# Mixers of a two-layer streaming encoder: six PSUM banks in one stock, a new task clock and projection order, and one score group for the later tokens

## The chip, the cores and the metric

The kernel runs on one core of one Trainium2 chip. The metric is the device time of one execution in microseconds (us), lower is better. The engines are TensorE (PE in the profile, with its weight loads as PEld), VectorE (DVE), ScalarE (ACT), GpSimd (POOL) and SyncE (SP), which here only issues DMAs. Each engine has its own list of instructions, in the order of the program, with waits on semaphores for the others.

## The reference, cut to what matters

Two layers, each a feed-forward block, a mixer and a second feed-forward block, for 256 prompt tokens and 32 later tokens (positions 512 to 543, with a cache of 512 keys and values). All matrices are fp32.

```python
x = x + 0.5 * swiglu(rmsnorm(x), ffn1)              # 1024 -> 2816 -> 1024
z = rmsnorm(x) @ w_in                               # 1024 -> 2560: q, k, v (4 heads), u, hc, bg, cg
q, k = rope(q), rope(k)
o = diff_attend(q, k, v)                            # softmax(q1 k1) - lam * softmax(q2 k2), times v
y_attn = rmsnorm(o, subln)                          # prompt: chunk mask; later tokens: 512 cached + 32 new keys
y_pool = pool_mix(u); y_conv = bg * short_conv(cg * hc)
x = x + concat(y_attn, y_pool, y_conv) @ w_out      # 1024 -> 1024
x = x + 0.5 * swiglu(rmsnorm(x), ffn2)
```

New keys, values and the states of pool and convolution are outputs too.

## The kernel before

Tokens lie in the free dimension (288 columns: 256 + 32), features in the 128 partitions. Every large product is made in three fp32r matmuls (`mm3`, lines 244 to 251): high weights by high input (L249), low weights by high input (L250), high weights by low input (L251). One such three is called a **triple** below. A block of 128 output features takes 8 triples where 1024 features go in. A mixer is 20 such blocks of w_in (its **projections**: q, k and v of four heads, two u, two hc, two bg, two cg), 160 triples, and then 64 triples of w_out.

Weights come from HBM in **chunks** of 1 MB, two projections each, three buffers deep. Each must be split into a high part (ACT, `wh`) and a low part (DVE, `wl` = raw - wh). In the mixers the split is made in four pieces of 128x512 for a chunk (pieces 0 to 3, each for four triples), one chunk ahead of its use (`split_task`, `chunk`). ACT and DVE share this work with everything else in the mixer.

That else is written as Python generators, **tasks**, that are started when a projection's accumulator is full (`after`): `rope` (four ACT copies `zw` of 32 partitions, z on DVE, zw times sin on POOL, then q or k on DVE), `val` (value times R, two transposes `tpv`, copy `vtk`), `attn_p` for a head (scores `sc`, maxima `nm` on DVE, four exponentials `e` on ACT, difference on DVE, transposes `tpa`, copy `aT`, product `o`, norm, transposes `tpo`, then mh on ACT and ml on DVE), `attn_s` for the later tokens of all heads (scores `scs`, `es_t`, `tps`, `os`), `pool` (`yp`), `conv` and `gate`. Each `yield wait(...)` is a place where the task may be left. A planner at build time sets the order: `main` emits a triple and moves `clock` on by a fixed cost, `poll` issues every task piece whose `ready_at` lies behind the clock, `Costed` charges each ACT, DVE and POOL instruction to a planned time of its engine. So the order of instructions on all engines is fixed when the kernel is built; on the chip, only semaphores decide. `IN_ORDER` gives the order of the projections (0 to 3 q, 4 to 7 k, 8 to 11 v, 12 and 13 u, 14 and 15 hc, 16 and 17 bg, 18 and 19 cg), and a list in the code the order in which w_out takes its eight inputs.

The kernel uses PSUM as eight banks of 128x512. Before, four rotate for accumulators (`ps_a`), two for tasks (`ps_t`), and `ps_s` holds a pair for scores. The feed-forward blocks use the same pools. In the first mixer, `lambdas` (ACT `lam_e`, DVE `nlam`) is issued when the first two projections are done.

Of the kernel before, what the change touches and what calls it, by code (L numbers as in the profile page):

```python
# [43 lines left out]
IN_ORDER = [0, 4, 1, 5, 8, 9, 2, 6, 10, 11, 3, 7, 14, 15, 12, 18, 13, 19, 16, 17]  # L44
# [20 lines left out]
def tile_step(ctx, tc, xT, head, w_gu, w_dn, w_in, w_out, rest, ck, cvp,  # L65
# [99 lines left out]
    def warm_up(n):  # L165

        warm = ps_a.tile([P, 512], F32, tag="acc", name="warm")
        for _ in range(n):
            PE.matmul(warm[:, 0:P], ones, ones, start=True, stop=True)
# [33 lines left out]
    def stats_a():  # L203

        ps = ps_t.tile([P, 512], F32, tag="tp", name="ps_ss")
# [14 lines left out]
    def stats_b(dg):  # L220
        ps = ps_t.tile([P, 512], F32, tag="tp", name="ps_r")
# [5 lines left out]
    def stats_wide():  # L227

        ps = ps_t.tile([P, 512], F32, tag="tp", name="ps_w")
# [23 lines left out]
    def acc_tile():  # L253
        return ps_a.tile([P, 512], F32, tag="acc", name="acc")
# [158 lines left out]
    def mixer(l, g_next):  # L413
        with tc.tile_pool(name="mp", bufs=1) as mp, tc.tile_pool(name="mt", bufs=2) as mt, \
# [24 lines left out]
            free = {"sc": [0.0], "tp": [0.0, 0.0]}  # L439
# [24 lines left out]

            def ready_at(t):
                _, res, _, dep = t[1]
                at = t[0]
                if dep is not None:
                    at = max(at, done.get(dep, never) + LAG)
                return max(at + MARGIN, min(free[res])) if res else at  # L470

            def issue(t, at):
                _, res, cost, _ = t[1]
                if res:
                    slots = free[res]
                    slots[slots.index(min(slots))] = never
# [4 lines left out]
            def release(res):  # L481
                slots = free[res]
                slots[slots.index(never)] = stage[1] + LAG
# [37 lines left out]
            class Costed:  # L521
# [3 lines left out]
                def __getattr__(self, op):  # L525
                    f = getattr(self.eng, op)

                    def call(out, *a, **kw):
                        n = max(a[0].free_size() if a and hasattr(a[0], "free_size") else 0, out.free_size())
                        if self.name == "act":  # L530
                            src = a[0]
                            c = (0.05 if src.space == PSUM else 0.1) + n / 1200.0 + (0.1 if "accum_out" in kw else 0.0)
                            c += sum(0.05 for x in ("scale", "bias") if hasattr(kw.get(x), "free_size"))
                        elif self.name == "dve":
                            c = 0.07 + n / 960.0
                        elif op == "tensor_tensor":
                            c = 0.3 + 0.165 * n if n < 4 else 0.1 + n * 0.0023
# [8 lines left out]
            def main(*a):  # L546
                mm3(*a)
                clock[0] += 0.369
# [29 lines left out]
            def stats():  # L578
                ps = ps_t.tile([P, 512], F32, tag="tp", name="ps_ss")
# [3 lines left out]
                V.tensor_scalar(a, ps[:, 0:3], 1.0 / D, EPS, ALU.mult, ALU.add)  # L583
                r = tmp.tile([P, 3], F32, tag="rs_r", name="rs_r")
# [6 lines left out]
                ps = ps_t.tile([P, 512], F32, tag="tp", name="ps_r")  # L591
# [5 lines left out]
                S.activation(R[0], ps[:, :T], AF.Copy)  # L597

            def rope(acc, h, isk):
# [6 lines left out]
                V.tensor_tensor(z, acc[:, :T], cosR, ALU.mult)  # L606
                G.tensor_tensor(zw, zw, sinR, ALU.mult)
# [11 lines left out]
            def val(acc, h):  # L619
                v = mt.tile([P, SEQ], F32, tag="vT", name="vT")  # L620
                V.tensor_tensor(v, acc[:, :SEQ], R[0][:, :SEQ], ALU.mult)
                V.tensor_tensor(vcat[:, h, :], acc[:, SEQ:T], R[0][:, SEQ:T], ALU.mult)
                nc.sync.dma_start(vT_o[l, h, :, 0:SEQ], v)
                nc.sync.dma_start(vT_o[l, h, :, SEQ:T], vcat[:, h, :])
                yield wait("tp", 0.45)
                tp = ps_t.tile([P, 512], F32, tag="tp", name="tpv")
# [5 lines left out]
                release("tp")  # L632
                mark(("v", h))

            def val_s():
                yield wait("tp", 0.22)
                tp = ps_t.tile([P, 512], F32, tag="tp", name="tpvs")
# [4 lines left out]
                release("tp")  # L642
                mark("vs")

            def attn_p(h):
# [33 lines left out]
                tp = ps_t.tile([P, 512], F32, tag="tp", name="tpa")  # L679
# [5 lines left out]
                release("tp")  # L685
                yield wait(dep=("v", h))
                yield wait("tp", 0.65)
                o = ps_t.tile([P, 512], F32, tag="tp", name="o")
# [6 lines left out]
            def finish(o, s1, n, dst, key):  # L695
# [16 lines left out]
                release("tp")  # L712
                yield wait("tp", 0.22 * n)
                tp = ps_t.tile([P, 512], F32, tag="tp", name="tpo")
# [10 lines left out]
                release("tp")  # L725
                mark(key)

            def attn_s():
                yield wait(dep=("q", 3))
                yield wait(dep=("k", 3))  # L730
                for c in range(2):
                    yield wait("sc", 1.0)
                    sc = ps_s.tile([P, 2, 512], F32, tag="sc", name="scs")
                    r = slice(64 * c, 64 * c + 64)
                    for b in range(2):
                        for h in range(H):
                            PE.matmul(sc[32 * h:32 * h + 32, b, 0:272], qT[h][r, SEQ:T],  # L737
                                      kts[r, h, b * 272:(b + 1) * 272], start=True, stop=True)
                    yield wait()
                    nm = mt.tile([P, 1], F32, tag="nms", name="nms")  # L740
                    V.tensor_reduce(nm, sc[:, :, 0:272], AX.XY, ALU.max)
                    V.tensor_scalar(nm, nm, -0.125, None, ALU.mult)
                    yield wait()
                    S.activation(es_t[:, c, :].rearrange("p (b k) -> p b k", b=2), sc[:, :, 0:272], AF.Exp,
                                 scale=0.125, bias=nm, accum_out=sms[:, c:c + 1])
                    release("sc")
                yield wait()
                fr = mt.tile([P, 1], F32, tag="frs", name="frs")
# [6 lines left out]
                tp = ps_t.tile([P, 512], F32, tag="tp", name="tps")  # L755
# [3 lines left out]
                tp2 = ps_t.tile([P, 512], F32, tag="tp", name="tps2")  # L759
# [3 lines left out]
                release("tp")  # L763
                release("tp")
                yield wait(dep="vs")
                yield wait("tp", 1.5)
                o = ps_t.tile([P, 512], F32, tag="tp", name="os")
# [8 lines left out]
            def pool(acc, g):  # L776
# [6 lines left out]
                V.tensor_tensor(e[:, 2 * HIST + SEQ:], acc[:, SEQ:T], R[0][:, SEQ:], ALU.mult)  # L783
                nc.sync.dma_start(pool_o[l, g, 0], e[:, SEQ:SEQ + HIST])
# [3 lines left out]
                w = mt.tile([P, L], F32, tag="ws", name="ws")  # L788
                w2 = mt.tile([P, L], F32, tag="ws2", name="ws2")
# [20 lines left out]
                yp = ps_t.tile([P, 512], F32, tag="tp", name="yp")  # L810
# [7 lines left out]
                release("tp")  # L818
                mark(("m", 4 + g))

            def times_R(acc, tag):
                t = mt.tile([P, T], F32, tag=tag, name=tag, bufs=1)
                V.tensor_tensor(t, acc[:, :T], R[0], ALU.mult)
                return t

            def conv(acc, g):
# [11 lines left out]
                y = mt.tile([P, L], F32, tag="ws", name="cy")  # L838
# [21 lines left out]
            def after(mi, acc):  # L860
# [12 lines left out]
                elif mi < 16:  # L873
                    hcR[mi - 14] = times_R(acc, f"hcR{mi - 14}")
# [5 lines left out]
            def residual(m, acc):  # L880
                V.tensor_tensor(xs[m], acc[:, :T], xs[m], ALU.add)
                yield wait()
# [16 lines left out]
            a2 = [acc_tile() for _ in range(2)]  # L899
# [13 lines left out]
            for i in range(2, 20, 2):  # L913
# [5 lines left out]
                for q in range(2):  # L919
                    acc = acc_tile()  # L920
# [3 lines left out]
            order = [4, 5, 0, 1, 2, 3, 6, 7]  # L924
            acc4 = [acc_tile() for _ in range(4)]
# [12 lines left out]
            for m in range(4, KD):  # L938
                if m % 2 == 0:
                    w = chunk()  # L940
                acc = acc_tile()
# [3 lines left out]
            finish_tasks()  # L945

    class Close:
# [11 lines left out]
        def sums_before(self):  # L959

            self.ps = ps_t.tile([P, 512], F32, tag="tp", name="ps_l")
# [8 lines left out]
        def finish_all(self, acc):  # L970
# [7 lines left out]
            half = [[acc_tile(), acc_tile()], [acc_tile(), ps_t.tile([P, 512], F32, tag="tp", name="yt_p")],  # L978
# [152 lines left out]
```

## Time and profile before

| what | before |
|---|---|
| median of 3 runs (lowest to highest) | 1077.22 us (1076.9 to 1078.23) |
| the profiled execution: its own time, its span | 1078.57 us, 1076.8 us |
| PE busy | 1064.5 us, 99% of the span |
| DVE, ACT, POOL busy | 698.5 us (65%), 534.2 us (50%), 32.1 us (3%) |
| granted clock of TensorE, mean | 0.998 of full speed |
| DMA | 180.11 MB, mean 167 GB/s |

The span is what the profile sees from the first to the last instruction. Matmuls overlap in the records (each shows about 0.29 us, one starts every 0.13 us), so a matmul's cost is read from starts, and an idle time that the profile shows for PE is less than what PE lost. The two mixers lie around 222 to 312 us and 752 to 842 us.

### The profile page before, as it was taken

To read this page: it belongs to the slowest core of one execution; us is meant where nothing else is said; L and a number is where in the kernel's file an instruction comes from. 1 tells how busy PE (TensorE), PEld (TensorE's weight loads), DVE (VectorE), ACT (ScalarE), POOL (GpSimd) and SP (SyncE) were. 2 spreads that over 40 slices of the span, in tenths; PEclk is the share of its full clock that TensorE was granted. 3 is DMA by queue.
4 is the path that set the end of the run, shared out by engine and by line. 5 is a ranking of instruction groups with operands and counts; after the bars stand their busy time and mean duration, and the time that the engine had idled before them with its cause. 6 is when DMAs were issued, how large, how long until landed. Compare 5 with 4: busy or idle time off the path is not lost.

```text
span 1076.8 us, 19610 instructions
## 1 busy us (share of the span) xinstructions
PE 1064.5 (99%) x8094; PEld 1053.0 (98%) x8094; DVE 698.5 (65%) x1195; ACT 534.2 (50%) x935; POOL 32.1 (3%) x61
## 2 busy tenths in 40 slices
PE   9999999999999999999999999999999999999997
PEld 8999999999999999999999999999999999999997
DVE  6866665557879666655576666554779786666442
ACT  6544444448665444444444444443785644444442
POOL 0000000011200000000000000000112000000000
PEclk9999999999999999999999999999999999999999
DMA  8664444444445444444445444544444364444421
GB/s 284 217 228 177 157 156 171 176 150 169 130 152 215 177 157 161 176 172 157 157 164 184 162 157 166 180 164 166 170 141 157 122 232 170 179 161 157 167 108 44
DMA packets 33417, 180.11 MB, mean 167 GB/s; under 512 B 7696, under 2 KB 10256, under 8 KB 12848
## 3 DMA queue, kind: packets, MB, share of 16 engines
q1 hardware_dynamic: 33328, 178.86, 47.2%
q8 instruction: 63, 1.03, 0.4%
q14 instruction: 26, 0.21, 0.0%
HBM read 175.24 MB, written 3.61 MB: 166 GB/s over the span
## 4 chain that ended last, share of the span: by engine, by line
PE 93%; ACT 3%; DVE 2%; DMA 1%; issue 1%; SPq 0%; POOL 0%; ACTq 0%; DVEq 0%; POOLq 0%
PE acc L249 29%; PE acc L251 29%; PE acc L250 29%; ACT zw L541 2%; DMA raw<-in_head 1%; ACT e L541 1%; PE sc L251 1%; PE sc L249 1%; PE sc L250 1%; ACT wh L541 0%; PE scs L737 0%; PE sc L651 0%; PE acc L299 0%; DVE wl L541 0%; PE os L772 0%
## 5 line engine op out<-in xcount | busy, mean ns | idle before, releaser
L249 PE MATMUL acc<-xh,wh 128*128 128x288 f32 x1632 | 487.2, 299 | 0.0
L250 PE MATMUL acc<-xh,wl 128*128 128x288 f32 x1632 | 480.8, 295 | 2.0 <-DVE wl L541 1.9
L251 PE MATMUL acc<-xl,wh 128*128 128x288 f32 x1632 | 480.3, 294 | 0.0
L109 DVE TENSOR_TENSOR wl<-raw,wh 128x1024 fp32r<-128x1024 f32 x258 | 315.7, 1224 | 188.4 <-ACT wh L108 188.0
L108 ACT ACTIVATE wh<-raw 128x1024 fp32r<-128x1024 f32 x258 | 273.1, 1060 | 290.1 <-PE acc L251 262.7
L250 PEld LDWEIGHTS acc<-xh,wl 128*128 128x128 f32 x1632 | 307.8, 189 | 3.9 <-DVE wl L541 3.1
L249 PEld LDWEIGHTS acc<-xh,wh 128*128 128x128 f32 x1632 | 306.7, 188 | 2.5 <-issue 1.4
L251 PEld LDWEIGHTS acc<-xl,wh 128*128 128x128 f32 x1632 | 306.8, 188 | 0.0
L249 PE MATMUL acc<-hh,wh 128*128 128x288 f32 x704 | 208.4, 296 | 0.0
L250 PE MATMUL acc<-hh,wl 128*128 128x288 f32 x704 | 207.7, 295 | 0.0
L251 PE MATMUL acc<-hl,wh 128*128 128x288 f32 x704 | 207.0, 294 | 0.0
L251 PEld LDWEIGHTS acc<-hl,wh 128*128 128x128 f32 x704 | 132.6, 188 | 0.0
L250 PEld LDWEIGHTS acc<-hh,wl 128*128 128x128 f32 x704 | 132.2, 188 | 0.0
L249 PEld LDWEIGHTS acc<-hh,wh 128*128 128x128 f32 x704 | 131.9, 187 | 0.0
L355 ACT ACTIVATE hh<-t 128x288 fp32r<-128x288 f32 x88 | 39.0, 444 | 108.0 <-DVE t L354 108.0
L541 DVE TENSOR_TENSOR wl<-raw,wh 128x512 fp32r<-128x512 f32 x112 | 76.6, 700 | 5.7 <-ACT wh L541 5.6
L541 ACT ACTIVATE wh<-raw 128x512 fp32r<-128x512 f32 x112 | 65.6, 627 | 6.5 <-PE acc L251 4.1
L356 DVE TENSOR_TENSOR hl<-t,hh 128x288 fp32r<-128x288 f32 x88 | 40.2, 458 | 39.7 <-ACT hh L355 39.4
L349 DVE TENSOR_TENSOR t<-acc,R 128x288 f32<-128x288 f32 x82 | 37.5, 457 | 31.6 <-PE acc L251 31.3
L352 ACT ACTIVATE t<-t 128x288 f32<-128x288 f32 x88 | 37.8, 429 | 6.8 <-DVE t L349 6.1
L354 DVE TENSOR_TENSOR t<-t,t 128x288 f32<-128x288 f32 x88 | 39.6, 451 | 0.1
L249 PE MATMUL acc<-mh,wh 128*128 128x288 f32 x128 | 37.9, 296 | 0.0
(215 smaller groups left out, 784.8 us busy)
## 6 DMA issues: line engine op xcount, KB each, us to landing
raw<-in_w_gu SPq DMA_DIRECT2D x85, 1024.0 KB, 4.8
raw<-in_w_dn SPq DMA_DIRECT2D x44, 1024.0 KB, 4.8
raw<-in_w_in SPq DMA_DIRECT2D x20, 1024.0 KB, 4.9
raw<-in_w_out SPq DMA_DIRECT2D x8, 1024.0 KB, 5.0
raw<-in_head SPq DMA_DIRECT2D x6, 528.0 KB, 6.8
kts<-in_ck SPq DMA_DIRECT2D x2, 1024.0 KB, 5.4
cvt<-in_cv SPq DMA_DIRECT2D x2, 1024.0 KB, 7.2
xall<-in_xT SPq DMA_DIRECT2D x1, 1152.0 KB, 9.9
```

Of the source, the lines that this page charges most:

```text
L108: S.activation(wh, src, AF.Copy)
L109: V.tensor_tensor(wl, src, wh.bitcast(F32), ALU.subtract)
L249: PE.matmul(acc, wh[:, b, :], mh, start=first, stop=False)
L250: PE.matmul(acc, wl[:, b, :], mh, start=False, stop=False)
L251: PE.matmul(acc, wh[:, b, :], ml, start=False, stop=last)
L349: V.tensor_tensor(t1, ag[:, :T], R, ALU.mult)
L352: S.activation(t1, t1, AF.Silu)
L354: V.tensor_tensor(h, t1, t2, ALU.mult)
L355: S.activation(hh[j], h, AF.Copy)
L356: V.tensor_tensor(hl[j], h, hh[j].bitcast(F32), ALU.subtract)
L541: return f(out, *a, **kw)
```

## The change

All of it is in the mixers and their planner.

- Six banks (`ps_b`, tags b0 to b5) form one stock. Accumulators, statistics and tasks take the bank that was free earliest (`take`, `taken`) and give it back by name (`release`), accumulators too, in the middle of a task. A task piece may only be planned while a second bank is free (`spare`). Outside the mixers the six are split four and two as before (`turn_of`, `next_bank`).
- The planner's costs are new: 0.4 instead of 0.369 for a triple, and other costs for ACT, DVE and POOL.
- `IN_ORDER` spreads the ropes: k0, v0, q0, hc0, u0, q1, k1, v1, q2, q3, k2, v2, cg0, k3, v3, bg0, u1, hc1, cg1, bg1. w_out takes its inputs as 4, 5, 6, 7, 2, 3, 0, 1.
- `attn_s` makes the scores of both halves of the heads (c = 0, 1) in one group: all 512 cached keys into the score pair, the 32 new keys into two banks of the stock (`scn`), copied by ACT to `sn`. Before, it was two groups, one for each half, each of 2 x 272 keys.
- Some SBUF buffers: one `ws`, `ws2`; `cy` with a buffer for each group.

```diff
-IN_ORDER = [0, 4, 1, 5, 8, 9, 2, 6, 10, 11, 3, 7, 14, 15, 12, 18, 13, 19, 16, 17]
+IN_ORDER = [4, 8, 0, 14, 12, 1, 5, 9, 2, 3, 6, 10, 18, 7, 11, 16, 13, 15, 19, 17]
+OUT_ORDER = [4, 5, 6, 7, 2, 3, 0, 1]
...
-    ps_a = ctx.enter_context(tc.tile_pool(name="ps_a", bufs=4, space=PSUM))
+    ps_b = ctx.enter_context(tc.tile_pool(name="ps_b", bufs=1, space=PSUM))
     ps_s = ctx.enter_context(tc.tile_pool(name="ps_s", bufs=1, space=PSUM))
-    ps_t = ctx.enter_context(tc.tile_pool(name="ps_t", bufs=2, space=PSUM))
...
+            def opening(res):
+
+                return sorted(free[res])[spare[0] if res == "tp" else 0]
...
-                return max(at + MARGIN, min(free[res])) if res else at
+                return max(at + MARGIN, opening(res)) if res else at
...
+            def taken(name):
+                b = bank(got[0], name)
+                held[id(b)] = (got[0], b)
+                return b
+
+            def take(name):
+
+                while min(free["tp"]) >= never:
+                    at, n = min((ready_at(t), n) for n, t in enumerate(tasks))
+                    assert at < never
+                    issue(tasks[n], at)
+                clock[0] = max(clock[0], min(free["tp"]))
+                got[0] = free["tp"].index(min(free["tp"]))
+                free["tp"][got[0]] = never
+                return taken(name)
...
-                            c = (0.05 if src.space == PSUM else 0.1) + n / 1200.0 + (0.1 if "accum_out" in kw else 0.0)
-                            c += sum(0.05 for x in ("scale", "bias") if hasattr(kw.get(x), "free_size"))
+                            c = 0.17 + n / 1200.0 + (0.1 if "accum_out" in kw else 0.0)
...
-                            c = 0.07 + n / 960.0
+                            c = max(0.18, 0.07 + n / 960.0)
...
-                clock[0] += 0.369
+                clock[0] += 0.4
...
+                yield wait("sc")
+                yield wait("tp")
+                tn = [taken("scn")]
+                yield wait("tp", 1.3)
+                tn.append(taken("scn"))
+                sc = ps_s.tile([P, 2, 512], F32, tag="sc", name="scs")
+                for dst, k0, n in ((tn, PAST, DEC), ([sc[:, 0, :], sc[:, 1, :]], 0, PAST)):
+                    for h in range(H):
+                        for c in range(2):
+                            r = slice(64 * c, 64 * c + 64)
+                            PE.matmul(dst[c][32 * h:32 * h + 32, 0:n], qT[h][r, SEQ:T], kts[r, h, k0:k0 + n],
+                                      start=True, stop=True)
+                yield wait()
+                sn = mt.tile([P, 2, DEC], F32, tag="sn", name="sn", bufs=1)
                 for c in range(2):
...
+                    S.activation(sn[:, c, :], tn[c][:, 0:DEC], AF.Copy)
+                    release(tn[c])
+                nm = mt.tile([P, 4], F32, tag="nms", name="nms")
+                V.tensor_reduce(nm[:, 0:2], sc, AX.X, ALU.max)
...
-            acc4 = [acc_tile() for _ in range(4)]
+            order = OUT_ORDER
+            acc4 = [take("acc") for _ in range(4)]
+            spare[0] = 0
```

Three places show how the order of instructions moves; both mixers are alike but for `lam_e`.

**Place 1, ACT at the start of the first mixer**, from the copy of the statistics (R) on. `zw x4` is one rope's share, a `wh` of 128x512 one piece of the next chunks' weights. Before:

```order
L541 ACTIVATE R<-ps_r 128x288
L541 ACTIVATE zw<-acc 32x288 x8
L273 ACTIVATE lam_e<-lam_s 128x4
L541 ACTIVATE wh<-raw 128x512
L541 ACTIVATE zw<-acc 32x288 x4
L541 ACTIVATE wh<-raw 128x512
L541 ACTIVATE zw<-acc 32x288 x4
L541 ACTIVATE wh<-raw 128x512 x3
```

Now, in the same stretch of ACT:

```order
L577 ACTIVATE R<-ps_r 128x288
L577 ACTIVATE zw<-acc 32x288 x4
L284 ACTIVATE lam_e<-lam_s 128x4
L577 ACTIVATE wh<-raw 128x512
L577 ACTIVATE zw<-acc 32x288 x4
L577 ACTIVATE vtk<-tpv 128x2x128
L577 ACTIVATE wh<-raw 128x512 x5
```

Four ropes stood ahead of the fifth piece of weights; now two do, and `lam_e` comes after one rope.

**Place 2, PE at the scores of the later tokens** (the numbers behind q are buffers of the four heads). Before, each mixer has two such groups, one for each half c:

```order
L737 MATMUL scs<-kts,q_2501 32x272
L737 MATMUL scs<-kts,q_2502 32x272
L737 MATMUL scs<-kts,q_2503 32x272
L737 MATMUL scs<-kts,q_2504 32x272
L737 MATMUL scs<-kts,q_2501 32x272
L737 MATMUL scs<-kts,q_2502 32x272
L737 MATMUL scs<-kts,q_2503 32x272
L737 MATMUL scs<-kts,q_2504 32x272
```

Now each mixer has one (x2: the two halves of a head, from partitions 0 to 63 and 64 to 127):

```order
L781 MATMUL scn<-kts,q_2498 32x32 x2
L781 MATMUL scn<-kts,q_2499 32x32 x2
L781 MATMUL scn<-kts,q_2500 32x32 x2
L781 MATMUL scn<-kts,q_2501 32x32 x2
L781 MATMUL scs<-kts,q_2498 32x512 x2
L781 MATMUL scs<-kts,q_2499 32x512 x2
L781 MATMUL scs<-kts,q_2500 32x512 x2
L781 MATMUL scs<-kts,q_2501 32x512 x2
```

The same columns of keys, in matmuls of 512 and 32 columns instead of 272, and the halves now alternate.

**Place 3, ACT after the scores of head 1**, now: the last exponentials of head 1, the rope of q2, piece 1 of chunk 5 (counted from 0; it holds the weights of k2 and v2), the rope of q3, then pieces 2 and 3 of chunk 5 and piece 0 of chunk 6:

```order
L577 ACTIVATE e,sm<-sc,nm 128x128
L577 ACTIVATE e,sm<-sc,nm 128x256
L577 ACTIVATE zw<-acc 32x288 x4
L577 ACTIVATE wh<-raw 128x512
L577 ACTIVATE zw<-acc 32x288 x4
L577 ACTIVATE wh<-raw 128x512 x3
```

Two ropes now stand close together here, each ahead of a piece of weights; before, q2 and q3 were four projections apart.


## Rows read from the trace of the kernel before

**Rows 1.** Page, busy time: us, share of the span, instructions of each engine.

```profile
PE 1064.5 (99%) x8094; PEld 1053.0 (98%) x8094; DVE 698.5 (65%) x1195; ACT 534.2 (50%) x935; POOL 32.1 (3%) x61
```

**Rows 2.** Windows: busy us (instructions) of a feed-forward stretch and a mixer.

```profile
222.00:312.00 90.00, 87.84 (x703) 82.94 (x702) 67.12 (x173) 59.61 (x165) 15.15 (x26) 1.00 0.47 161
312.00:752.00 440.00, 440.00 (x3323) 439.78 (x3323) 280.71 (x415) 201.20 (x285) 0.00 (x0) 1.00 0.47 167
```

**Rows 3.** Timeline of PE, mixer 1: start, us, instruction [idle <-releaser].

```profile
232.34 0.29 PE L251 MATMUL acc<-xl,wh 128*128 128x288 f32 x1
...
234.04 0.40 PE L250 MATMUL acc<-xh,wl 128*128 128x288 f32 x1 [1.07 <-DVE wl L541]
234.28 0.30 PE L251 MATMUL acc<-xl,wh 128*128 128x288 f32 x1
...
238.24 0.29 PE L249 MATMUL acc<-xh,wh 128*128 128x288 f32 x1
...
238.87 0.29 PE L251 MATMUL acc<-xl,wh 128*128 128x288 f32 x1
...
241.79 0.29 PE L249 MATMUL acc<-xh,wh 128*128 128x288 f32 x1
...
242.21 0.29 PE L251 MATMUL acc<-xl,wh 128*128 128x288 f32 x1
243.18 0.71 PE L651 MATMUL sc<-k,q 64*128 64x256 f32 x4 [0.68 <-ACT e L541]
...
255.06 0.29 PE L249 MATMUL acc<-xh,wh 128*128 128x288 f32 x1
...
255.92 0.30 PE L251 MATMUL acc<-xl,wh 128*128 128x288 f32 x1
```

**Rows 4.** Timeline of PE, mixer 2, first lost stretch.

```profile
766.34 0.29 PE L249 MATMUL acc<-xh,wh 128*128 128x288 f32 x1
...
767.02 0.30 PE L251 MATMUL acc<-xl,wh 128*128 128x288 f32 x1
```

**Rows 5.** Waits of PE in 752 to 842 us: us in total, times, longest.

```profile
PE sc L651 <- ACT e L541: 0.7, 1, 0.7
PE acc L250 <- DVE wl L541: 0.5, 2, 0.3
```

**Rows 6.** Timeline of ACT, start of mixer 1.

```profile
227.62 3.32 ACT L541 ACTIVATE zw<-acc 32x288 f32<-32x288 f32 x8
```

**Rows 7.** Timeline of DVE, the same stretch.

```profile
231.20 0.64 DVE L274 TENSOR_TENSOR nlam<-lam_e 128x2 f32<-128x2 f32 x1 [3.44 <-ACT lam_e L273]
...
233.31 0.68 DVE L541 TENSOR_TENSOR wl<-raw,wh 128x512 fp32r<-128x512 f32 x1
```

**Rows 8.** Timeline of PE, a score group of later tokens and their product os.

```profile
277.97 0.29 PE L251 MATMUL acc<-xl,wh 128*128 128x288 f32 x1
278.19 1.12 PE L737 MATMUL scs<-kts,q 64*32 64x272 f32 x16
279.25 0.41 PE L249 MATMUL acc<-xh,wh 128*128 128x288 f32 x1
279.49 0.29 PE L250 MATMUL acc<-xh,wl 128*128 128x288 f32 x1
...
294.85 1.08 PE L772 MATMUL os<-cvt,aTs 128*32 128x128 f32 x32
295.86 0.42 PE L772 MATMUL os<-vsm,aTs 32*32 32x128 f32 x8
```

**Rows 9.** Timeline of DVE, maxima of a prompt head.

```profile
239.63 0.42 DVE L541 MEMSET sc<- 64x128 f32 x2
...
241.14 0.17 DVE L541 TENSOR_SCALAR nm<-nm 128x4 f32<-128x4 f32 x1
```

**Rows 10.** Timeline of ACT, exponentials of that head and four pieces of weights.

```profile
241.41 0.37 ACT L541 ACTIVATE e<-sc,nm 128x128 f32<-128x128 f32 x1 [2.63 <-DVE nm L541]
...
243.01 2.19 ACT L541 ACTIVATE wh<-raw 128x512 fp32r<-128x512 f32 x4
```

More of the change, by code (lines that the diff above doesn't have):

```diff
@@ L74, in tile_step, with bank, next_bank @@
     tmp = ctx.enter_context(tc.tile_pool(name="tmp", bufs=2))
[L75 removed]
+    ps_b = ctx.enter_context(tc.tile_pool(name="ps_b", bufs=1, space=PSUM))
     ps_s = ctx.enter_context(tc.tile_pool(name="ps_s", bufs=1, space=PSUM))
[L77 removed]
+    turn_of = {"acc": [0, 1, 2, 3], "tp": [4, 5]}
+    def bank(i, name):
+        return ps_b.tile([P, 512], F32, tag=f"b{i}", name=name)
+    def next_bank(kind, name):
+        ids = turn_of[kind]
+        ids.append(ids.pop(0))
+        return bank(ids[-1], name)
     chunks = []
@@ L438, in mixer @@
             clock = [0.0]
-            free = {"sc": [0.0], "tp": [0.0, 0.0]}
+            free = {"sc": [0.0], "tp": [0.0] * 6}
+            held = {}
+            got = [0]
+            spare = [1]
             never = 1e9
@@ L479, in issue, with release @@
                 advance(t, at)
-            def release(res):
-                slots = free[res]
-                slots[slots.index(never)] = stage[1] + LAG
+            def taken(name):
[11 more added lines that the diff above has]
+                return taken(name)
+            def release(b):
+                if b == "sc":
+                    free["sc"][0] = stage[1] + LAG
+                else:
+                    free["tp"][held.pop(id(b))[0]] = stage[1] + LAG
             def mark(key):
@@ L578, in stats @@
             def stats():
-                ps = ps_t.tile([P, 512], F32, tag="tp", name="ps_ss")
+                ps = take("ps_ss")
                 for b, (t0, _, _) in enumerate(TB):
@@ L590, in stats @@
                 yield wait()
-                ps = ps_t.tile([P, 512], F32, tag="tp", name="ps_r")
+                ps = take("ps_r")
                 PE.matmul(ps[:, :T], ones, dg, start=True, stop=True)
@@ L730, in attn_s @@
                 yield wait(dep=("k", 3))
-                for c in range(2):
[L732 to L746, printed above, removed]
@@ new lines, in attn_s @@
+                V.tensor_scalar(nm[:, 0:2], nm[:, 0:2], -0.125, None, ALU.mult)
+                yield wait()
+                for c in range(2):
+                    S.activation(es_t[:, c, 0:PAST], sc[:, c, :], AF.Exp, scale=0.125, bias=nm[:, c:c + 1],
+                                 accum_out=sms[:, c:c + 1])
+                release("sc")
+                for c in range(2):
+                    S.activation(es_t[:, c, PAST:], sn[:, c, :], AF.Exp, scale=0.125, bias=nm[:, c:c + 1],
+                                 accum_out=sms[:, 2 + c:3 + c])
@@ L748, in attn_s @@
+                yield wait()
+                V.tensor_tensor(sms[:, 0:2], sms[:, 0:2], sms[:, 2:4], ALU.add)
                 fr = mt.tile([P, 1], F32, tag="frs", name="frs")
@@ L754, in attn_s @@
                 yield wait("tp", 0.87)
-                tp = ps_t.tile([P, 512], F32, tag="tp", name="tps")
+                tp = taken("tps")
                 for b in range(4):
@@ L898, in mixer @@
             w = chunk()
-            a2 = [acc_tile() for _ in range(2)]
+            a2 = [take("acc") for _ in range(2)]
             for q in range(2):
@@ L919, in mixer @@
                 for q in range(2):
-                    acc = acc_tile()
+                    acc = take("acc")
                     for k in range(KD):
@@ L940, in mixer @@
                     w = chunk()
-                acc = acc_tile()
+                acc = take("acc")
                 for k in range(KD):
@@ L945, in mixer @@
             finish_tasks()
+            ids = sorted(range(6), key=lambda i: free["tp"][i])
+            turn_of["acc"], turn_of["tp"] = ids[:4], ids[4:]
     class Close:
```

70 lines of the change are left out of this document (40 added, 30 removed).

## The prediction

> **What bounds the kernel now.** I read the page first: PE is busy for 99% of the span, DVE for 65%, ACT for 50% [rows 1]. Then a table of windows: in a long stretch outside the mixers PE has no idle time at all and starts a matmul every 440.00 / 3323 = 0.132 us (a triple every 0.397 us); in a mixer's 90 us ACT has work for 60 and DVE for 67 [rows 2]. So ACT and DVE have time enough over a mixer as a whole; only their order can make PE wait. The change leaves the triples as they are, so it can win only what PE loses inside the mixers: waits, and the price of task pieces.
>
> What PE waits for is in its timeline. As matmuls overlap in the records, the view of waits shows too little; I take the time from the start ahead of a wait to the start after it, less 0.132 for each step between. Mixer 1 [rows 3]: 232.34 to 234.28 is 1.94 for three steps, 1.54 lost, on low weights from DVE; 238.24 to 238.87, 0.37 lost; 241.79 to 242.21, 0.16; 242.21 to 243.18, 0.97, where the step into a score group without a wait takes 0.22 (277.97 to 278.19, [rows 8]), so 0.75 lost, on the exponentials of head 0, which still hold the score pair; 255.06 to 255.92, 0.60. Sum 3.42. Mixer 2: the first place loses 0.68 - 0.26 = 0.42 [rows 4], and the view of waits has the same 0.7 for the score pair and two short waits for weights [rows 5]; I take the other three places as in mixer 1 (0.16, 0.75, 0.60), sum 1.93. Together **5.35 us**.
>
> Why they arise: at the start ACT copies eight `zw` for two ropes, 3.32 us [rows 6]. In mixer 1 `lam_e` stands behind them, and DVE, in its order, stands at `nlam` for 3.44 us before it may make the low weights that PE needs, from 233.31 on [rows 7]. All five losses fall in the stretch with ropes 0, 4, 1, 5, 2, 6 close together.
>
> **The change part by part.**
>
> *New order of projections, and the planner's costs.* 0.4 for a triple is nearer to the 0.397 of [rows 2] than 0.369 was; with the old one the planner believed that PE comes sooner than it does. I followed the new order by hand with the durations of the rows: a rope's four `zw` 3.32 / 2 = 1.66 [rows 6], a piece of high weights 2.19 / 4 = 0.55, exponentials 243.01 - 241.41 = 1.60 [rows 10], maxima from 239.63 to 241.31, 1.68 [rows 9], low weights 0.68 [rows 7].
>
> Place 1, start of mixer 1: ACT begins the first rope at 227.62 as before, ends it at 229.28, `lam_e` at about 229.5. DVE took 2.11 from `nlam` to the low weights with three rope steps between [rows 7]; now one is there, so they start at the latest at 229.5 + 2.11 = 231.6 and end at 232.3. PE came to these weights at about 232.5 [rows 3], and now has one pair of transposes more ahead of them. The 1.54 (and the 0.42 of mixer 2) is gone, by a margin of 0.2 with this late bound. The third and fourth rope now come at the sixth and seventh projection instead of the third and fourth, so the 0.37, 0.16 and 0.75 lose their cause too: the score group of head 1 now comes 31 triples after that of head 0 instead of 14, and its pair has long been given back.
>
> Place 3 is the tight one. From the start of head 1's scores to the first use of piece 2 of chunk 5, PE has 19 triples, 7.54, and task pieces: scores 1.0, four pairs and threes of transposes 0.8 (an estimate from the column price below), 9.3 in all, and the low weights are wanted one step later, 9.5. The other chain: scores 0.8, maxima 1.68, exponentials 1.60, rope q2 1.66, piece 1 0.55, rope q3 1.66, piece 2 0.55, low weights 0.68, sum 9.2, and some six hand-offs of 0.05 to 0.1 between engines (241.31 to 241.41, [rows 9, 10]), 9.5 to 9.8. So PE waits between nothing and 0.5; I take **0.25 lost in each mixer**, a new wait. In the other chunks I find each piece ready 0.5 us or more before its first triple. Where a DVE instruction now stands waiting for a projection (values, bg), low weights are queued behind it, but for a later chunk. Taken together the new order gives back 5.35 - 0.5 = **4.85 us**; from below, with 1 us of new waits in each mixer, 3.35; from above 5.35.
>
> *Scores of later tokens.* A group cost 277.97 to 279.49, 1.52 less two steps, 1.26 us; a mixer has two, 2.51. For the price of columns: four heads run side by side, a matmul takes two records, so a group is four rounds of 272 columns in 279.25 - 278.19 = 1.06, and os eight rounds of 128 in 1.01 [rows 8]; the line through both is 0.78 ns for a column plus 0.21. The new group has two rounds of 512 if all eight (head, half) run side by side, 1024 columns, 1.01 like os. The new keys add between 0.05 (64 columns) and 0.42 (the short group of os); I take 0.15. With the steps in and out as before (0.09 and 0.11) the group costs 1.36: a saving of 1.16 in a mixer, **2.3 us** in both. If the two halves don't run side by side, four rounds of 512, 1.8, leave 2.2 for the group and a saving of only 0.3. No row shows eight at once; os shows four column places, the prompt scores two row places (four records of 256 columns in 0.71 us, where 4 x 256 x 0.78 ns one after another are 0.80 and the length of the last, [rows 3]), so I take eight. The Trainium skill (TensorE: Matmul & The Clock Gate, the part on packing small matmuls) says that row and column places compose, with a measured gain of 10.6 for sixteen; by it the sum is the same 1.16, and no run here shows it yet.
>
> *Evacuation.* Two copies `sn`, two more exponentials and three more small DVE steps come behind the new group, and both halves' exponentials in one. Between the group and `tps` PE has 15 triples, 6.0 us, and two task pieces; the chain (maxima of 1024 columns, two exponentials of 512 and two of 32, difference) is an estimate of 5 us from the rows of a prompt head (1.68 and 1.60 for 768). It costs nothing while that cover of about 1 us or more holds; without it `tps`, and all main triples behind it on PE, wait.
>
> *The stock of banks.* It adds waits of PE for a bank. A bank is held for 3.2 us by a projection's triples (8 x 0.397), 1.66 by the rope's copies and somewhat more by z, and a projection starts every 3.2 us, so some two of six are in use, plus short tasks. I count nothing, up to 0.5 in a mixer. The new DMA order is harmless as far as I see: loads still wait for a buffer to be split, as before.
>
> **Sum.** 4.85 + 2.3 = 7.15. The profiled execution would go from 1078.57 to 1071.4; it lies 1.35 above the median of the runs, so the median goes from 1077.22 to about **1070.0**.
>
> **The rivals.**
> 1. *The halves of the scores don't run side by side* (speaks for it: the program alternates them, which no row shows; against: place by place they do). 4.85 + 0.6 = 5.45: 1071.8.
> 2. *Waits come back elsewhere.* The work of ACT and DVE is the same, and a hand count of some two hundred instructions can miss a place where a piece of weights stands behind a task. The Trainium skill (TensorEngine Tiling (Array Packing), PSUM bottleneck) warns that a faster TensorE leaves the evacuation of PSUM as the limit; here that is the chain behind the merged scores, and by that rule the saving of the scores would be lost at `tps`. The mechanism: if that chain takes 2 us longer than estimated, PE waits 1 us or more in each mixer, and with as much again for weights 3 us are given back: 1073.
> 3. *Nothing is won*: the planner's order matters less than the total, and 5 us of waits move to other places: within 0.2%, 1075 to 1079. Against: the losses have named causes that the new order removes.
> 4. *Slower: PE waits for banks.* Projections and tasks now take from one stock; where the bank is given back by a DVE or ACT step that stands behind low weights, a projection begins late. It needs 7.15 + 2.2 = 9.35 us, 0.23 for each of 40 projections, before the kernel is slower by 0.2%; at one piece of low weights (0.68) for every second one, 13.6, the time is 1083.7. Against: two or three of six banks in use.
>
> **How the numbers follow.** The forecast has 0.70 (its own range 1068.9 to 1071.3), rival 1 0.08, rival 2 0.13, rival 3 0.06, rival 4 0.03. A change under 0.2% (2.2 us) can't be told from none here, the three runs alone spread over 1.3 us. Faster is the first three, 0.91; same 0.06; slower 0.03. Range: from no new wait and scores at the lower bound (5.35 + 2.5, 1069.4, and 0.6 for what I can't see) to rival 2: 1068.8 to 1073.4.
>
> **What would show it right or wrong.** In the new profile PE should wait for low weights and for exponentials for under 0.5 us in each mixer, the largest of it at piece 2 of chunk 5; one score group of later tokens in a mixer, some 1.2 to 1.4 us from the step before it to the step after; the pace outside the mixers the same 0.132. It is wrong if PE waits at `tps`, at a projection's first matmul (a bank), or if the scores take four rounds.

## The result and the profile after

| | median of the runs | ratio to before, 95% interval | mixer 1 | mixer 2 |
|---|---|---|---|---|
| before | 1077.0 us (1076.9 to 1078.23) | | 109.45 us | 107.97 us |
| after | 1071.79 us (1071.22 to 1072.34) | 0.9949 (0.9935 to 0.9964) | 105.89 us | 105.88 us |

The change saves 5.2 us in the medians. A mixer is measured from the first start of `ps_ss` in it to that of `ps_w` in the feed-forward block behind it; these lengths repeat to about 0.1 us from one profile to the next, so I use them below more than the medians. Measured so, the mixers of before reach to 332 and 860 us, further than the 312 and 842 named above, as the output projection belongs to them. Both mixers together got shorter by 5.65 us.

The page and the windows answer to [rows 1, 2]. First the page of after, then the windows of its two mixers with the stretch between them, then the same two windows of before (length, then busy us and instructions of PE, PEld, DVE, ACT, POOL, granted clock, DMA share, GB/s).

```profile
PE 1061.1 (99%) x8094; PEld 1052.1 (98%) x8094; DVE 696.7 (65%) x1197; ACT 537.0 (50%) x947; POOL 37.3 (3%) x61
```

```profile
220.88:326.77 105.89, 105.45 (x849) 101.76 (x848) 83.62 (x209) 76.72 (x202) 17.73 (x26) 1.00 0.49 159
326.77:746.97 420.20, 420.20 (x3174) 419.99 (x3173) 263.08 (x381) 185.42 (x255) 0.00 (x0) 1.00 0.49 169
746.97:852.86 105.89, 105.63 (x850) 101.69 (x849) 83.50 (x206) 76.62 (x201) 17.74 (x26) 1.00 0.50 160
```

```profile
222.60:332.04 109.44, 107.28 (x849) 102.38 (x848) 84.25 (x208) 75.72 (x196) 15.15 (x26) 1.00 0.44 149
752.25:860.21 107.96, 106.79 (x849) 102.25 (x848) 83.72 (x205) 75.65 (x195) 15.16 (x26) 1.00 0.46 152
```

ACT and DVE have as much to do as before. In both mixers together PE's idle time fell from 3.33 to 0.70 us and its busy time by 2.99. The pace between the mixers is 420.20 / 3174 = 0.132 us, as before.

The two profiled executions differ by more, 1078.57 to 1071.22. Of that, 1.7 us lie ahead of mixer 1, in code that did not change. About 1.0 of it is a wait of PE early in the first feed-forward block, which the profile of before has and that of after has not; the other 0.7 lies ahead of that wait. That wait does not come from the change: the instructions of experiments 4 and 11 are the same, and the profile of 4 has the wait where that of 11 has not. PE's timeline of before:

```profile
30.55 0.75 PE L222 MATMUL ps_r<-rs_d,ones 128*128 128x288 f32 x2 [0.72 <-DVE rs_d L217]
```

All places of [rows 3, 4] have lost their waits. What PE waits for now is nearly all low weights. The view of waits, PE's weight loads, 222 to 330 us, has one row of `acc` behind `wl` (total us, times, longest):

```profile
PEld acc L261 <- DVE wl L577: 0.7, 1, 0.7
```

It is the place the prediction called Place 3: piece 2 of chunk 5, behind head 1's exponentials and the ropes of q2 and q3. PE's timeline there:

```profile
257.61 0.32 PE L260 MATMUL acc<-xh,wh 128*128 128x288 f32 x1
258.36 0.40 PE L261 MATMUL acc<-xh,wl 128*128 128x288 f32 x1 [0.44 <-DVE wl L577]
258.60 0.30 PE L262 MATMUL acc<-xl,wh 128*128 128x288 f32 x1
```

By the prediction's own rule, 0.99 for two steps, 0.73 lost. Counted likewise, with the ends of the matmuls, mixer 1 loses 0.71 here, 0.14 at piece 2 of chunk 7 and 0.06 twice (once of them for `ml`), 0.97 in all; mixer 2 loses 0.39 and 0.41 at pieces 1 and 2 of chunk 5, 0.13 and 0.05, 0.98. No projection waits for a bank, and nothing waits at `tps`.

The one score group of later tokens, which answers to [rows 8], in PE's timeline:

```profile
283.85 0.30 PE L262 MATMUL acc<-xl,wh 128*128 128x288 f32 x1
284.07 0.27 PE L781 MATMUL scn<-kts,q 64*32 64x32 f32 x13
284.16 0.59 PE L781 MATMUL scs<-kts,q 64*32 64x512 f32 x1
...
284.18 1.05 PE L781 MATMUL scs<-kts,q 64*32 64x512 f32 x13
285.16 0.49 PE L730 MATMUL o<-vtk,aT 128*128 128x128 f32 x2
```

From the step before it to the step after it 1.31 us. The 16 records of 512 columns come in two rounds of eight, which start 0.43 us apart (one record takes 0.59, the row of 13 merged ones 1.05): all eight pairs of head and half run side by side.

### The profile page after: what moved, and what is told of

Read it like the earlier page. It is cut to its first block, busy times and chain, and to the rows that moved or that the text cites. A ratio compares the mean times of both kernels' runs of the same rounds, so it can differ in the third digit from the quotient of the medians.

```text
span 1069.4 us, 19633 instructions
## 1 busy us (share of the span) xinstructions
PE 1061.1 (99%) x8094; PEld 1052.1 (98%) x8094; DVE 696.7 (65%) x1197; ACT 537.0 (50%) x947; POOL 37.3 (3%) x61
## 4 chain that ended last, share of the span: by engine, by line
PE 97%; ACT 1%; DMA 1%; DVE 0%; issue 0%; SPq 0%; ACTq 0%
PE acc L260 30%; PE acc L261 30%; PE acc L262 30%; PE acc L310 1%; PE sc L262 1%; PE sc L260 1%; PE sc L261 1%; ACT zw L577 1%; DMA raw<-in_head 1%; PE sc L691 0%; PE sc L310 0%; ACT e L577 0%; PE os L827 0%; PE o L730 0%; ACT wh L577 0%; PE tpv L668 0%
```

## The experiments

"Mixers" are the two lengths defined above; the ratio is to before, with its 95% interval. Where a diff says `-`, that is the changed kernel, unless said otherwise. In experiments 3, 5, 7, 8 and 11 the output projection also asks for the later tokens' product already ahead of inputs 2 and 3, which read it too, and not only ahead of 0 and 1. With the old prices and clock this changes nothing: the kernels of experiments 4 (without it) and 11 (with it) issue the same instructions in the same order.

**1. The old score groups.** In `attn_s`, shortened:

```diff
-                for dst, k0, n in ((tn, PAST, DEC), ([sc[:, 0, :], sc[:, 1, :]], 0, PAST)):
...
+                for c in range(2):
+                    yield wait("sc", 1.0)
...
+                                PE.matmul(sc[32 * h:32 * h + 32, b, 0:272], qT[h][r, SEQ:T],
```

> The changed kernel with the old two score groups of later tokens (each of four rounds of 272 columns, with its own step in and out) in place of the merged one; all else as after the change. The prediction's theory, corrected by the trace of after (the one group costs 1.31 us, and one of 1.26 is saved, less 0.05 for more columns): each mixer gets longer by 1.2 us, the kernel by 2.4, 1074.2. Rival 1 (the two halves don't run side by side, so that merging saves only 0.3 in each mixer): 1072.4. Rival 2 (the chain behind the merged scores costs as much as the merging saves): no change, 1071.8.

1073.6 us, 0.9969 (0.9958 to 0.998); mixers 107.05 and 107.09, longer by 1.16 and 1.21. PE's timeline has the two groups again:

```profile
280.51 1.12 PE L777 MATMUL scs<-kts,q 64*32 64x272 f32 x16
286.56 1.12 PE L777 MATMUL scs<-kts,q 64*32 64x272 f32 x16
```

The 1.16 of the prediction stands; both rivals of this term fall.

**2. Only the new order, on the kernel before.**

```diff
-IN_ORDER = [0, 4, 1, 5, 8, 9, 2, 6, 10, 11, 3, 7, 14, 15, 12, 18, 13, 19, 16, 17]
+IN_ORDER = [4, 8, 0, 14, 12, 1, 5, 9, 2, 3, 6, 10, 18, 7, 11, 16, 13, 15, 19, 17]
+OUT_ORDER = [4, 5, 6, 7, 2, 3, 0, 1]
```

> The kernel before with nothing but the new order of input and output projections; its prices, its clock, its banks and its two score groups are the old ones. The prediction put the whole 4.85 us of waits on order and prices together. If the order does it alone, the mixers get shorter by 2.5 and 1.0 us (3.42 and 1.93 lost before, less about 0.95 of new waits in each), 1073.5. If it needs the true prices too, half or less of that: 1075 to 1077. If it needs the common stock (two banks for tasks are too few in this order), mixers are as long as before or longer.

1072.94 us, 0.9962 (0.9948 to 0.9977); mixers 106.81 and 106.82, together 3.79 shorter than before. With the old prices PE does not wait for low weights at all. What it loses instead is 0.5 at the first score group of later tokens, for exponentials that still hold the pair, and some 0.1 at each of two groups of transposes. PE's timeline:

```profile
279.54 1.12 PE L738 MATMUL scs<-kts,q 64*32 64x272 f32 x16 [0.45 <-ACT e L542]
```

So the order gives 3.79 by itself, on the kernel before, and the merging 2.37 (1.16 + 1.21), on the kernel after. Prices, clock, stock and buffers, the step from here to experiment 1, cost 0.51 (213.63 to 214.14). The sum is 5.65. These shares hold for this order of steps: taken away last, in experiment 4, the new prices and clock cost more.

**3. The banks apart.** Four banks for accumulators in turn, two for tasks:

```diff
-            free = {"sc": [0.0], "tp": [0.0] * 6}
+            free = {"sc": [0.0], "tp": [0.0, 0.0]}
...
-                b = bank(got[0], name)
+                b = bank(4 + got[0], name)
```

> The changed kernel with the banks apart as before: four for accumulators, taken in turn and not planned for, two for tasks; order, prices and scores as after the change. The prediction counted the stock at nothing: within 0.3 us of the changed kernel. If tasks need more than two banks in the new order (the merged scores hold two by themselves), the attention's transposes and products come later, PE waits for the last of them ahead of the output projections, and each mixer gets longer by 0.5 to 2 us, 1073 to 1076.

1088.67 us, 1.0113 (1.0098 to 1.0128); mixers 115.56 and 115.57: 9.7 longer each, worse than either theory. The merged scores take two banks at once, and with only two for all tasks they start at 292.79 instead of 284.07. The output projection then finds its operands late: PE waits 2.30 us for `ml` from DVE, and 11 us later 1.7 us for `on` from ACT, the later tokens' product. PE's timeline, and the granted clock (the number ahead of the DMA share) in two windows behind it:

```profile
292.79 0.27 PE L775 MATMUL scn<-kts,q 64*32 64x32 f32 x13
...
298.67 0.40 PE L262 MATMUL acc<-ml,wh 128*128 128x288 f32 x1 [2.30 <-DVE ml L571]
...
299.70 0.40 PE L260 MATMUL acc<-mh,wh 128*128 128x288 f32 x1
299.90 0.44 PE L261 MATMUL acc<-mh,wl 128*128 128x288 f32 x1
300.14 0.44 PE L262 MATMUL acc<-ml,wh 128*128 128x288 f32 x1
```

```profile
299.70:302.60 2.90, 2.90 (x16) 2.88 (x14) 2.43 (x5) 0.08 (x1) 0.00 (x0) 0.51 0.47 195
310.60:316.50 5.90, 5.84 (x23) 5.67 (x24) 0.68 (x2) 0.01 (x1) 0.00 (x0) 0.50 0.51 178
```

A second loss comes with each of these two waits: in the stretch behind it the granted clock is 0.51 and 0.50, which is 1.2 instead of 2.4 GHz, and a step takes 0.24 us instead of 0.13. Whether the stock is needed without the merged scores was not tried; experiment 2, with the old banks and the old score groups, has no such waits.

**4. The old prices and the old clock.**

```diff
-                            c = 0.17 + n / 1200.0 + (0.1 if "accum_out" in kw else 0.0)
+                            c = (0.05 if src.space == PSUM else 0.1) + n / 1200.0 + (0.1 if "accum_out" in kw else 0.0)
+                            c += sum(0.05 for x in ("scale", "bias") if hasattr(kw.get(x), "free_size"))
...
-                            c = max(0.18, 0.07 + n / 960.0)
+                            c = 0.07 + n / 960.0
...
-                            c = 0.75 + 0.165 * n if n < 4 else 0.15 + n * 0.0026
+                            c = 0.3 + 0.165 * n if n < 4 else 0.1 + n * 0.0023
...
-                clock[0] += 0.4
+                clock[0] += 0.369
```

> The changed kernel with the planner's old prices and its old clock of 0.369 us for a triple; order of projections, stock of banks and scores as after the change. If the order of projections alone gave the waits back, PE's waits stay as they are, 1.0 us in each mixer, and the time is within 0.5 us of the changed kernel's. If the true prices are what keeps the pieces of weights ahead of PE, old waits return: between 1 and 2.5 us in each mixer, 1074 to 1077.

1070.04 us, 0.9935 (0.992 to 0.995); mixers 104.56 and 104.54. No theory had a gain: the waits for weights are gone. At Place 3 ACT now makes a piece of weights ahead of the first rope. ACT's timeline of this kernel:

```profile
252.66 0.21 ACT L578 ACTIVATION_READ_ACCUMULATOR e<-sc,nm 128x1 f32 x1
252.75 0.64 ACT L578 ACTIVATE wh<-raw 128x512 fp32r<-128x512 f32 x1
253.41 1.64 ACT L578 ACTIVATE zw<-acc 32x288 f32<-32x288 f32 x4
255.08 0.63 ACT L578 ACTIVATE wh<-raw 128x512 fp32r<-128x512 f32 x1
255.74 1.64 ACT L578 ACTIVATE zw<-acc 32x288 f32<-32x288 f32 x4
```

And that of after:

```profile
252.60 0.21 ACT L577 ACTIVATION_READ_ACCUMULATOR e<-sc,nm 128x1 f32 x1
252.84 1.65 ACT L577 ACTIVATE zw<-acc 32x288 f32<-32x288 f32 x4
254.51 0.63 ACT L577 ACTIVATE wh<-raw 128x512 fp32r<-128x512 f32 x1
255.17 1.64 ACT L577 ACTIVATE zw<-acc 32x288 f32<-32x288 f32 x4
256.84 1.67 ACT L577 ACTIVATE wh<-raw 128x512 fp32r<-128x512 f32 x3
```

**5. The old clock alone.**

```diff
-                clock[0] += 0.4
+                clock[0] += 0.369
```

> The changed kernel with only the planner's clock put back (0.369 us for a triple instead of 0.4; prices, order, stock and scores as after the change; the later tokens' product is asked for one chunk earlier in the output projections, which only matters if it is late). With both old numbers (prices and clock) the time was 1070.04 and the mixers 104.55 us instead of 105.9. If the old clock is what keeps the pieces of weights ahead of the rope copies: mixers of 104.6, 1070.0. If it is the prices: mixers of 105.9 or longer, 1071.8 or more.

1134.86 us, 1.0538 (1.0522 to 1.0553); mixers 139.08 and 135.54. With the new, higher prices and the slow clock pieces of weights come late all through the mixer, and tasks behind them. PE's weight loads in mixer 1, in the view of waits:

```profile
PEld acc L261 <- DVE wl L577: 10.2, 9, 2.1
PEld o L730 <- DVE ml L577: 4.5, 1, 4.5
```

The waits are not all of the loss. In four stretches of mixer 1, 27 us together, the granted clock is 0.50 as well. The longest of them, in the view of windows:

```profile
311.00:324.60 13.60, 7.65 (x51) 5.07 (x52) 8.36 (x20) 7.46 (x24) 0.69 (x1) 0.50 0.45 154
```

**6. The old prices alone** (experiment 4 without its last edit, the clock).

> The changed kernel with only the old prices put back (clock 0.4 as after the change; order, stock and scores too). If the new prices are what puts a piece of weights behind two ropes: mixers of 104.6, 1070.0. If the clock is: mixers of 105.9, 1071.8. If either of them suffices, both of these runs are at 1070.0; if the place of each piece hangs on small differences of times in the planner, the mixers lie between 104.5 and 107 with no order in it.

1077.11 us, 1.0001 (0.9992 to 1.0011); mixers 108.26 and 108.20. Here no weights are late, but PE comes to tasks before they are ready. PE's waits in mixer 1:

```profile
PE tpa L722 <- DVE e L578: 0.9, 2, 0.6
PE tps L813 <- DVE es_t L578: 0.8, 1, 0.8
PE yp L868 <- DVE pd L578: 0.7, 1, 0.7
```

Neither old number gives what both give: with the one pieces of weights come too late, with the other tasks too early. What counts is prices against clock.

**7. A clock of 0.43, with the new prices.**

```diff
-                clock[0] += 0.4
+                clock[0] += 0.43
```

> The changed kernel with the planner's clock at 0.43 us for a triple, further from the 0.397 that a triple takes than 0.4 is; its prices are the new ones. If what counts is prices against clock (new prices with 0.369 were far too late, old prices with 0.4 too early, both old or both new about right), a clock that is faster by 7% brings every piece forward: behind head 1's exponentials a piece of weights now stands before the rope, the waits for weights go, and the mixers take 104.5 to 105.3 us, 1069 to 1070.6. If it brings too much forward, PE waits for tasks as with the old prices and 0.4: mixers of 107 to 108, 1074 to 1077. If a clock that is true to the chip is best, it is slower than 0.4 in any case.

1069.31 us, 0.9932 (0.9918 to 0.9946); mixers 104.91 twice, without a wait for weights. The clock is further from the true 0.397, and the mixers are 0.98 shorter than after the change: that a clock true to the chip is best falls.

**8. Weights booked 0.6 us earlier**, the rest as after:

```diff
-                        yield wait()
+                        yield (-0.6, None, 0.0, None)
                         S.activation(wh[:, sl, :], src, AF.Copy)
```

> The changed kernel with every piece of high weights booked 0.6 us earlier in the planner; its prices, its clock of 0.4, order, stock and scores are those after the change. Behind head 1's exponentials ACT now makes one piece of weights, then a rope, one piece, and a rope, in place of a rope, one piece, a rope, one piece. If the wait of after is only that piece's place behind the rope (1.66 us), it goes, and the mixers take 104.5 to 104.9 us: 1069.7 to 1070.5. If pieces that come earlier put a task late in their place (scores, transposes or the output projection), the mixers stay at 105.9 or get longer: 1071.8 or more.

1069.56 us, 0.9937 (0.992 to 0.9954); mixers 105.20 and 105.21. The waits for weights are gone, so the piece's place behind the rope was their cause. Some of it is given back, about 0.45 in each mixer, at the output projection, where `mh` and `ml` now come later.

**9. Without GpSimd's product in the ropes.**

```diff
-                G.tensor_tensor(zw, zw, sinR, ALU.mult)
+                charge("pool", 0.15 + T * 0.0026)
```

> The changed kernel without GpSimd's product of zw and sinR in the ropes (part of the computation is left out; the planner still charges it, so the order of everything else is the same). In the trace of after a subtraction for low weights takes 0.68 us, but 0.74 to 0.81, and once 1.14, where it starts while this product runs. If the subtraction waits there until the product has ended, all of them take 0.68 now, the wait at piece 2 of chunk 5 is 0.58 in mixer 1 and at most 0.28 in mixer 2, those at chunk 7 are gone, and the mixers get shorter by 0.27 and 0.65 us, 1070.9. If the longer records are only long in the records, nothing changes: 1071.8, with the same waits.

1071.07 us, 0.9947 (0.9933 to 0.9962); mixers 105.69 and 105.73. All low weights take 0.68 now. The group of the 54 in mixer 2 (min, median, max in ns), first after, then this kernel:

```profile
L577 DVE TENSOR_TENSOR wl<-raw,wh x54: 678/684/1137, 747.8 to 849.5; 128x512 fp32r<-128x512 f32 x54
```

```profile
L577 DVE TENSOR_TENSOR wl<-raw,wh x54: 677/684/693, 747.3 to 848.8; 128x512 fp32r<-128x512 f32 x54
```

So a subtraction did wait for the product. But of the 0.27 and 0.65 us expected only 0.20 and 0.16 came: in each mixer one wait of 0.60 is left at piece 2 of chunk 5 (in mixer 2 that at piece 1 went, and the next grew). The hold-off is the smaller part of the new wait, the piece's place the larger.

**10. The loops of the merged scores exchanged.**

```diff
                     for h in range(H):
                         for c in range(2):
+                    for c in range(2):
+                        for h in range(H):
```

> The changed kernel with the two loops of the merged scores exchanged: first the four heads of one half, then the four of the other, so that the program no longer alternates between the two row places. In after all eight pairs of head and half start within 0.02 us of each other and the group costs 1.31 us. If that needs the alternation, the halves come one after the other, four rounds of 512 columns instead of two, and the group costs 0.8 us more: mixers of 106.7, 1073.4. If any free place of the array takes the next matmul in line, nothing changes: mixers of 105.9, 1071.8.

1071.62 us, 0.9951 (0.9937 to 0.9964); mixers 105.83 and 105.85. The alternation is not needed: still two rounds, with the same starts.

**11 and 12. Old prices and clock beside the changed kernel, with more runs.**

> The changed kernel with the planner's old prices and old clock together, once more, next to the changed kernel itself and with more runs (the same program as the first such run). Its mixers took 104.55 us against 105.89, so it should stay ahead by 2.7 us, 1069.1 where the changed kernel has 1071.8. If the first result was a lucky median, both come out within 0.5 us of each other.

> The changed kernel as it is, beside the one with the old prices and clock: 1071.8, mixers of 105.9 us, 1.0 us of waits for low weights in each. If the waits for weights hang on chance (how a DMA or GpSimd falls), they are at other places or of another size in this profile.

Old prices and clock: 1069.91 us, 0.9935 (0.9923 to 0.9948), mixers 104.57 and 104.63. The changed kernel: 1072.26 us, 0.9954 (0.9941 to 0.9968), mixers 105.81 twice, its waits at the same four places. So they do not hang on chance, and the old numbers win 2.4 us in the mixers. Some 0.9 of that is lost again: in both profiles of this program PE stands ahead of mixer 2, at its first projection. In the timeline of experiment 4:

```profile
742.94 0.38 PE L260 MATMUL acc<-xh,wh 128*128 128x288 f32 x1 [0.64 <-DVE xall L415]
```

The releaser is the addition that reads the feed-forward block's last accumulators, so this looks like a wait for a bank, as in the fourth rival: a mixer starts with the first two banks of the stock, whichever the block before used last. That was not tried apart, and neither was a start with the two banks that are free longest. The versions of experiments 4, 7, 8 and 11 have shorter mixers than the changed kernel, by 0.6 to 1.4 us each, and lower medians. The intervals of their ratios overlap with one another, and with that of the changed kernel too, so on the whole time I don't rank them.

## Why the prediction was right, and where it was off

- **The time.** 1070.0 was forecast, 1071.79 measured: inside the range, but above the likeliest case's own range. In the mixers 5.65 us were won of 7.15, which is the prediction's bound from below, 3.35 + 2.3, with 1 us of new waits in each mixer. The time is also the 1071.8 of rival 1, by chance: the scores do run side by side, and what is missing was lost on weights. With the old prices and clock the mixers are 8.2 to 8.3 shorter than before (experiments 4 and 11), more than the 7.15.
- **The five lost waits** (5.35 us): right. None of their places has a wait now.
- **The new wait at Place 3: the step that failed**, "I take 0.25 lost in each mixer". The place is right, the size was 0.97 and 0.98 per mixer, 0.7 to 0.8 of it at chunk 5; the prediction's own sign, under 0.5 in each mixer, did not hold. These rows show how (ACT's are in experiment 4), DVE's timeline and POOL's:

```profile
257.50 0.81 DVE L577 TENSOR_TENSOR wl<-raw,wh 128x512 fp32r<-128x512 f32 x1 [0.20 <-ACT wh L577]
258.23 0.44 DVE L577 TENSOR_TENSOR q<-z,zw 128x288 f32<-128x288 f32 x1
258.60 0.68 DVE L577 TENSOR_TENSOR wl<-raw,wh 128x512 fp32r<-128x512 f32 x1
```

```profile
256.96 0.81 POOL L577 TENSOR_TENSOR zw<-zw,sinR 128x288 f32<-128x288 f32 x1 [1.52 <-ACT zw L577]
```

  From the scores' start at 248.33 PE came to these weights after 9.4 us (9.5 predicted), but the chain took 10.0 (9.5 to 9.8). Scores to the first DVE step took 1.04 (0.8 predicted), exponentials 1.72 (1.60), a piece of high weights behind a rope 0.63 twice (0.55 is the pace inside a row of four, where one overlaps the next), low weights 0.81 (0.68); hand-offs only 0.2 in all. Chunk 7's 0.13 had been counted as "ready 0.5 us or more before".
- **Who made that wait**: also wrong. The text credits order and prices together, since 0.4 "is nearer to the 0.397". Order alone gave 3.79 us (experiment 2), and with old prices and clock there is no wait for weights (experiments 4, 11): the new prices together with the clock of 0.4 made it.
- **Scores of later tokens**: 1.16 in each mixer predicted, 1.16 and 1.21 by experiment 1. What the Trainium skill (TensorE: Matmul & The Clock Gate, packing small matmuls) says, that row and column places compose, the trace now shows: eight 64x32 pieces in one round.
- **Evacuation and rival 2**: nothing waits at `tps`. The chain behind the merged scores took 5.7 us from PE's next step (285.16) where 5 were estimated, and ended 1.5 us before `tps`; DVE's and PE's timeline:

```profile
290.08 0.79 DVE L577 SCALAR_TENSOR_TENSOR es_t<-es_t,frs 128x544 f32<-128x544 f32 x1
```

```profile
292.39 0.38 PE L812 MATMUL tps<-ident,es_t 128*128 128x128 f32 x2
```

  So the warning of the Trainium skill (TensorEngine Tiling (Array Packing), PSUM Bottleneck) has no effect here. But small waits did come back elsewhere, 0.7 in each mixer beyond the 0.25 of the forecast, where rival 2's 3 us are 1.5 in each. (That sum is off as written: 1 us and as much again in each of two mixers is 4.)
- **The stock of banks**, counted at nothing: right as a cost, wrong as a description. Without it the changed kernel, whose merged scores hold two banks, is slower by 16.9 us (1088.67 to 1071.79).
- **Rival 3** falls; **rival 4**, a wait for banks, shows at most in the versions with the old prices, once for 0.9 us (that this is a wait for a bank is not shown).

## What to carry to other kernels

Where a planner weighs prices against a clock, the two together place the pieces, so change and measure the two together, and look after each change at which side waits: weights (too late) or tasks (too early). Price a chain by the latency of each link, not by the pace of a row of the same instructions, wherever the next link stands behind another task. An edit that seems to add nothing may carry the one beside it: take parts away singly before calling one of them free.

## What the runs showed of the hardware

- DVE's `wl` and GpSimd's `zw` product, both with two operands in SBUF, hold each other up. In mixer 2 of after, DVE's and then POOL's timeline:

```profile
781.26 1.14 DVE L577 TENSOR_TENSOR wl<-raw,wh 128x512 fp32r<-128x512 f32 x1 [0.20 <-ACT wh L577]
...
783.59 0.81 DVE L577 TENSOR_TENSOR wl<-raw,wh 128x512 fp32r<-128x512 f32 x1 [0.20 <-ACT wh L577]
```

```profile
781.05 0.81 POOL L577 TENSOR_TENSOR zw<-zw,sinR 128x288 f32<-128x288 f32 x1 [6.76 <-ACT zw L577]
783.04 0.81 POOL L577 TENSOR_TENSOR zw<-zw,sinR 128x288 f32<-128x288 f32 x1 [1.19 <-ACT zw L577]
```

  The first ends 1.14 - 0.68 = 0.46 late and the second 0.13 late: each runs its full 0.68 from about 0.14 before the recorded end of the product. The other way round the product waits, at 240.38 for 1.27 instead of 0.81, behind a `wl` that began 0.08 earlier. The Trainium skill (SBUF — State Buffer, Who interferes with whom) says that a DVE instruction with two SBUF inputs contends with a GpSimd instruction that reads SBUF, and that the order of issue decides which of them blocks. The trace agrees for these two. GpSimd's power of two columns (`nf`), two operands in SBUF too, held up no `wl`: one that starts 0.44 into its record of 1.09 (at 247.56) takes 0.68. That record itself starts behind another `wl`, so part of it may be waiting.
- A wait of PE can cost twice: in experiment 3 an idle 2.30 us was followed, 1.0 us later, by at least 2.9 us in which the granted clock was 0.51. A wait of 0.72 us in the profile of before, and the 0.44 of Place 3, left it at 1.00.
